# A sevenfold projection whose operand pieces, gates and sums share one ring of ten tiles, with its last two units interleaved

## The chip, the cores and the metric

The kernel runs on one core of a Trainium2 chip. The metric is the device time of one execution in microseconds, and a version is judged by the median of several executions. One more execution was taken with the hardware profiler, and the times of single instructions come from it.

## What is computed

One layer of a decoder block for 1024 tokens of width 1024 in float32. Two mixers read the same normalised input: a dilated attention, which gives `o_a`, and a retention, which gives `o_r`. Each is projected to the model's width, the two are gated and added, and an output projection and an MLP follow:

```python
y = jax.nn.sigmoid(gate_a) * (o_a @ w_proj_a[l]) + jax.nn.sigmoid(gate_b) * (o_r @ w_proj_b[l])
x = x + y @ w_out[l]
xn2 = rmsnorm(x, norm2_g[l])
x = x + jnp.square(jax.nn.relu(xn2 @ w_up[l])) @ w_down[l]
```

The change lies in the stage that computes `o_r @ w_proj_b` (2048 by 1024 weights), the second gating and the sum `y`.

## The kernel before

**Products.** Float32 accuracy is made from two halves of each operand: `split` (L320, L321) lets ScalarE copy a tile into a rounded high half (names that end in h) and VectorE subtract it for the low half (names that end in l). A product of two operands is then three matmuls for each 128 rows of the contraction, high by high and the two mixed ones. `Pipe.group` (L223) issues them; all matmuls of the trace have that line.

**Sevenfold units.** The stage multiplies by a Strassen scheme: 8 units j of 7 products N1 to N7, each of 4 contraction steps and 3 matmuls, 12 matmuls of 128x512 in all, so 56 products. Units 0 to 3 handle one half of the contraction and units 4 to 7 the other, so that unit j + 4 adds to the results of unit j. A unit gives four results of 128x512, at N2, N7, N4 and N3. `product` issues one product and what follows it. Three PSUM banks of a unit gather the sums: one in pool `mm` for N1 and N2, one in pool `ms` for N6, N7 and N4, one in `mm` for N5 and N3. Between the products stand copies that TensorE must wait for:

- after N1, ScalarE copies the negated bank to the `ms` bank (L387); N2 overwrites its bank only after that;
- after N6, ScalarE copies its bank to `u2` (L392); N7 waits for it, since it adds to that bank;
- after N7, ScalarE copies to `u3` (L395), which N4 waits for, and VectorE subtracts the third bank from `u3` (L396), which N3 waits for, since it overwrites that bank;
- after N3, VectorE subtracts `u2` from the bank (L401).

`u2` and `u3` come from the pool `pub`, one buffer each.

**Operands.** The other operand of each product, 2 x 7 sums of parts of `o_r`, was put into DRAM (`on_d`) by the stage before. The stage loads it while it runs, in pieces: `load_sum` (DMA at L786, tile `oraw`, 512 KB) requests half an operand, and `part_sum` splits it (128x1024, one instruction on ScalarE and one on VectorE). A piece is requested after each product if fewer than two are open, and split two products after its request. Pool `pr2` has two tiles. Operands for units 0 to 3: N4, N3 and for units 4 to 7: N1 are loaded first, and each product of unit 3 sets its buffer free for the next operand of units 4 to 7 (the table `after`).

**Weights.** `Weights` streams `w_pb_q` through raw tiles (L176) and splits them on ScalarE and VectorE; the sums that the scheme needs on the weights' side are VectorE's at L121.

**Results.** The gated part of the first projection, `pa`, lies in DRAM (`pa_d`). A result of units 0 to 3 is either stored as it is to `pb_d` (through a ScalarE copy if it stands in PSUM, L1020), or gated with a tile of `sg_d` and added to one of `pa_d`, then stored to `pb_d` (L1029 to L1032). Which results are stored as they are is decided by `f == i`: N2 and N7. A result of units 4 to 7 is completed with what lies in `pb_d` (L1025 to L1030), and split for the output projection (`keep`); the first of each goes by way of `yl_d` in DRAM. `fetch` requests gates and sums two results ahead, into tiles `s` of the pool `pm3`, seven tiles of 256 KB, in which a request waits for the last reader of the tile seven requests back.

**Queues.** All DMAs of the stage are issued on SyncE (SP) in program order, so a write to DRAM that waits for its data holds up the loads behind it. ScalarE and VectorE also work in the order that the scheduler fixed when the kernel was built. TensorE runs the products in the order of the list `order`: for units 0 to 5, N6, N5, (j+2, N1), N7, (j+2, N2), N4, N3; for the last two units, N6, N5, N7, N3, N4 with nothing between. Behind the stage comes the output projection (`w_out`), whose weight tiles are split into buffers that a table of numbers picks.

Of the kernel before, what the change touches and what calls it, by code (L numbers as in the profile page):

```python
# [269 lines left out]
def hybrid_block(ctx: ExitStack, tc: tile.TileContext, a: dict, out: bass.AP):  # L270
# [18 lines left out]
    sg_d = dram.tile([2, KT, P, S], F, name="sg_d")  # L289
# [67 lines left out]
    for nb in range(2):  # L357
        for u in range(4):
            W.add(a["w_out"][nb, u], (4, 3, 2, 5)[u] if nb else (2, 5, 0, 1)[u])
# [334 lines left out]
    todo = []  # L694
# [253 lines left out]
    with ExitStack() as ph:  # L948
# [35 lines left out]
        pr = pool(ph, "pr2", 2)  # L984
        pub = pool(ph, "pub", 1)
        pm3 = pool(ph, "pm3", 7)
        order = [(0, "N1"), (1, "N1"), (0, "N2"), (1, "N2")]
        for j in range(8):
            more_n = [(j + 2, name) for name in ("N1", "N2")] if j < 6 else []
            order += [(j, "N6"), (j, "N5"), *more_n[:1], (j, "N7"), *more_n[1:]]  # L990
            order += [(j, name) for name in (("N4", "N3") if j < 6 else ("N3", "N4"))]
# [4 lines left out]
        def fetch(n):  # L996

            if n >= len(results):
                return
            j, f, i = results[n]  # L1000
            d, cs = 2 * (j % 4) + f, halves()[i]
            if j < 4 and f == i:
                return
            srcs = [sg_d[1], pa_d] if j < 4 else [sg_d[1], pb_d] + [pa_d] * (f == i)
            ahead[n] = [loaded(pm3, src[d, :, cs], "s") for src in srcs]
# [35 lines left out]
        todo, unit = [(c, name, h) for c, name in ((0, "N4"), (0, "N3"), (1, "N1")) for h in range(2)], {}  # L1041
        begun = []
        fetch(0)
        fetch(1)
        for i, (j, name) in enumerate(order):
            product("pb", j, name, unit, OPB[j // 4], lambda: pub, result)
            todo += [(1, after[j, name], h) for h in range(2) if (j, name) in after]
            if begun and begun[0][0] <= i - 2:
                _, c, op, h, raw = begun.pop(0)
                part_sum(OPB[c][op], raw, h)  # L1050
            if todo and len(begun) < 2:
                begun.append((i, *todo[0], load_sum(pr, *todo.pop(0))))
            if (j, name) in free:
                u = free[j, name]
                lo, _ = halves()
                keep(u, 0, lo, late.pop(u))
            if (j, name) in fetched:
                u = fetched[j, name]
                late[u] = loaded(pm3, yl_d[u - 4], "s")
# [369 lines left out]
```

## Time and profile before

| | |
|---|---|
| median of 3 runs | 2264.69 us (2263.36 to 2267.54) |
| profiled execution | 2264.52 us, of which the span on the core is 2262.8 |
| TensorE busy | 2217.5 us, 98% of the span |
| VectorE, ScalarE, GpSimd busy | 1349.2, 1046.1, 399.4 us |
| data moved | 311.64 MB, mean 138 GB/s |

Over the whole span TensorE is all but full. The stage of the 56 products runs from 1357.52 (its first matmul) to 1529.38 (the first matmul of the output projection), 7.6% of the span, and moves 43.38 MB at a mean of 248 GB/s, so the core's DMA engines work far harder there than on average. A row of the timeline gives start, duration, engine, line, operation and tile; in square brackets stands the idle time of the engine before it and the instruction that ended it. A row of the groups gives the number of instructions, their busy time and the mean of one in ns, then the idle time before them by releaser.

### The profile page before, as it was taken

The page shows a single profiled execution, that of the slowest core. Times are in us where ns is not written, and L with a number is a line of the kernel's source. Part 1 is how long each engine was busy: PE and PEld are TensorE (multiplying, and loading weights), DVE is VectorE, ACT ScalarE, POOL GpSimd, SP SyncE. Part 2 cuts the span into 40 slices and gives each one's busy share as a digit, 9 for nine tenths or more (in the row PEclk, how much of TensorE's full clock was granted, in tenths as well). Part 3 has the DMA queues.
Part 4 walks back from the last instruction along what each step waited for, and adds up shares of the span by engine and source line. Part 5 has one row for each costly group of instructions (what it writes and reads, how often), then busy time and mean ns, then how long its engine had stood idle before and what let it go on. Part 6 is the DMA issues. An engine that isn't in the chain of part 4 may idle for free. (4 is left out here: it accounts for less than half of the span.)

```text
span 2262.8 us, 30601 instructions
## 1 busy us (share of the span) xinstructions
PE 2217.5 (98%) x10772; PEld 1897.1 (84%) x10772; DVE 1349.2 (60%) x2552; ACT 1046.1 (46%) x2334; POOL 399.4 (18%) x436
## 2 busy tenths in 40 slices
PE   8999999999999999999999999989999999899999
PEld 7999999998888888888888877778788888778777
DVE  6444545455544445558677767783855556787874
ACT  6444435345333333335555634432555555654542
POOL 1111111110000000002132220000000000587873
PEclk9999999999999999999999999999999999999999
DMA  4313232322233333353464487763345556644532
GB/s 150 97 52 106 64 92 87 92 85 99 84 111 104 108 111 109 113 178 119 128 187 121 120 268 262 262 223 135 107 133 151 152 153 199 224 152 168 178 120 103
DMA packets 247565, 311.64 MB, mean 138 GB/s; under 512 B 15090, under 2 KB 171122, under 8 KB 247411
## 3 DMA queue, kind: packets, MB, share of 16 engines
q1 hardware_dynamic: 247410, 309.69, 42.2%
q8 instruction: 84, 1.38, 0.2%
q14 instruction: 71, 0.57, 0.1%
HBM read 209.92 MB, written 99.71 MB: 137 GB/s over the span
## 5 line engine op out<-in xcount | busy, mean ns | idle before, releaser
L321 DVE TENSOR_TENSOR wl<-raw,wh 128x1024 fp32r<-128x1024 f32 (+2 forms) x290 | 318.3, 1101 | 368.8 <-ACT wh L320 367.8
L223 PE MATMUL mm<-wh,xh 128*128 128x384 f32 (+1 forms) x1226 | 481.8, 393 | 0.6 <-DVE Y L1269 0.5
L223 PE MATMUL mm<-wh,xl 128*128 128x384 f32 (+1 forms) x1226 | 438.9, 358 | 1.7 <-DVE xl L321 1.6
L223 PE MATMUL mm<-wl,xh 128*128 128x384 f32 (+1 forms) x1226 | 437.5, 357 | 0.0
L320 ACT ACTIVATE wh<-raw 128x1024 fp32r<-128x1024 f32 (+2 forms) x290 | 273.3, 945 | 348.3 <-PE ms L223 116.3
L223 PE MATMUL mm<-xh,wh 128*128 128x512 f32 x720 | 283.1, 393 | 8.8 <-DVE u L396 5.7
L223 PE MATMUL mm<-xl,wh 128*128 128x512 f32 x720 | 282.4, 392 | 1.7 <-DVE xl L321 1.7
L223 PE MATMUL ms<-xh,wh 128*128 128x512 f32 x700 | 276.7, 395 | 5.5 <-ACT u L395 2.6
L223 PE MATMUL mm<-xh,wl 128*128 128x512 f32 x720 | 282.1, 392 | 0.0
L223 PE MATMUL ms<-xl,wh 128*128 128x512 f32 x700 | 273.3, 390 | 0.0
L223 PE MATMUL ms<-xh,wl 128*128 128x512 f32 x700 | 273.1, 390 | 0.0
L223 PEld LDWEIGHTS mm<-wh,xl 128*128 128x128 f32 x1226 | 230.7, 188 | 21.9 <-DVE xl L321 2.7
L223 PEld LDWEIGHTS mm<-wh,xh 128*128 128x128 f32 x1226 | 231.8, 189 | 19.9 <-DVE Y L1269 1.3
L223 PEld LDWEIGHTS mm<-wl,xh 128*128 128x128 f32 x1226 | 232.6, 190 | 16.7
L223 PEld LDWEIGHTS mm<-xh,wh 128*128 128x128 f32 x720 | 136.4, 189 | 38.9 <-DVE u L396 6.5
L223 PEld LDWEIGHTS mm<-xl,wh 128*128 128x128 f32 x720 | 136.3, 189 | 30.2 <-DVE xl L321 2.2
L223 PEld LDWEIGHTS ms<-xh,wh 128*128 128x128 f32 x700 | 131.9, 188 | 35.3 <-ACT u L395 4.5
L223 PEld LDWEIGHTS mm<-xh,wl 128*128 128x128 f32 x720 | 136.4, 189 | 28.5
L223 PEld LDWEIGHTS ms<-xh,wl 128*128 128x128 f32 x700 | 131.8, 188 | 27.7
L223 PEld LDWEIGHTS ms<-xl,wh 128*128 128x128 f32 x700 | 131.9, 188 | 26.4 <-DVE xl L321 0.2
L334 POOL TENSOR_TENSOR ssa<-ssa,half 128x2 f32<-128x2 f32 x96 | 66.7, 695 | 426.5 <-DVE ssa L333 409.6
L872 POOL TENSOR_TENSOR st<-st,half 128x1 f32<-128x1 f32 x32 | 27.5, 858 | 646.7 <-DVE st L871 641.4
(300 smaller groups left out, 3659.3 us busy)
## 6 DMA issues: line engine op xcount, KB each, us to landing
raw<-in_w_att SPq DMA_DIRECT2D x48, 384.0 KB, 3.8
raw<-in_w_up SPq DMA_DIRECT2D x32, 512.0 KB, 3.8
h_d<-s SPq DMA_DIRECT2D x64, 256.0 KB, 4.3
raw<-in_w_down SPq DMA_DIRECT2D x32, 512.0 KB, 3.8
oraw<-on_d SPq DMA_DIRECT2D x28, 512.0 KB, 4.9
s<-sg_d SPq DMA_DIRECT2D x40, 256.0 KB, 4.1
xh<-h_d SPq DMA_DIRECT2D x11, 896.0 KB, 4.3
xl<-h_d SPq DMA_DIRECT2D x10, 896.0 KB, 4.7
```

Source lines behind the costliest of these rows:

```text
L223: self.nc.tensor.matmul(ps, x, y, start=start, stop=stop, skip_group_check=not first)
L320: nc.scalar.activation(dst_h, src, AF.Copy)
L321: nc.vector.tensor_tensor(dst_l, src, dst_h.bitcast(F), op=OP.subtract)
L334: nc.gpsimd.tensor_tensor(dst, dst, half[:, :w], op=OP.pow)
L872: nc.gpsimd.tensor_tensor(st[:, 9:10], st[:, 8:9], half[:, 0:1], op=OP.pow)
```

## The change

Four things change in this stage, and a table of numbers behind it.

- *One ring.* The pools `pr2` (two tiles of 512 KB) and `pm3` (seven tiles of 256 KB) become one `pm3` of ten tiles of 256 KB, 2.5 MB instead of 2.75. Pieces of operands, gates, sums and copies of results take its tiles in turn. `u2` gets two buffers.
- *Smaller pieces.* An operand is loaded in four pieces of 256 KB instead of two of 512 KB (36 pieces instead of 18), up to two of them requested after each product, up to six open, and split three products after the request instead of two.
- *Which results are stored as they are:* `f`, that is N7 and N4 instead of N2 and N7.
- *Order of products:* units 0 to 5 as before; of the last two, each product but for the ends now stands beside one of the other unit.
- *Behind the stage*, the first two of the four weight tiles of `w_out`'s first half swap their buffers, and the last two of its second half.

```diff
@@ -356,7 +356,7 @@
     W.add_units("pb", [a["w_pb_q"][j] for j in range(8)])
     for nb in range(2):
         for u in range(4):
-            W.add(a["w_out"][nb, u], (4, 3, 2, 5)[u] if nb else (2, 5, 0, 1)[u])
+            W.add(a["w_out"][nb, u], (4, 3, 5, 2)[u] if nb else (5, 2, 0, 1)[u])
     NU, RING = FF // 256, 10
     W.add_units("up", [a["w_up"][j] for j in range(NU)])
     NC = FF // 512
@@ -981,14 +981,19 @@
         assert not waiting
         load.close()
         YS = [XS[0, 0], XS[1, 0], ES[0], ES[1]]
-        pr = pool(ph, "pr2", 2)
         pub = pool(ph, "pub", 1)
-        pm3 = pool(ph, "pm3", 7)
+
+        class parts:
+            @staticmethod
+            def tile(shape, dtype, name):
+                return pub.tile(shape, dtype, name=name, bufs=2 if name == "u2" else 1)
+
+        pm3 = pool(ph, "pm3", 10)
         order = [(0, "N1"), (1, "N1"), (0, "N2"), (1, "N2")]
-        for j in range(8):
-            more_n = [(j + 2, name) for name in ("N1", "N2")] if j < 6 else []
-            order += [(j, "N6"), (j, "N5"), *more_n[:1], (j, "N7"), *more_n[1:]]
-            order += [(j, name) for name in (("N4", "N3") if j < 6 else ("N3", "N4"))]
+        for j in range(6):
+            order += [(j, "N6"), (j, "N5"), (j + 2, "N1"), (j, "N7"), (j + 2, "N2"), (j, "N4"), (j, "N3")]
+        order += [(6, "N6"), (6, "N5"), (6, "N7"), (7, "N6"), (6, "N4"), (7, "N5"), (7, "N7"), (6, "N3"), (7, "N4"),
+                  (7, "N3")]
         results = [(j, *{"N2": (0, 0), "N7": (1, 1), "N4": (1, 0), "N3": (0, 1)}[name])
                    for j, name in order if name in ("N2", "N7", "N4", "N3")]
         ahead, late = {}, {}
@@ -999,9 +1004,9 @@
                 return
             j, f, i = results[n]
             d, cs = 2 * (j % 4) + f, halves()[i]
-            if j < 4 and f == i:
+            if j < 4 and f:
                 return
-            srcs = [sg_d[1], pa_d] if j < 4 else [sg_d[1], pb_d] + [pa_d] * (f == i)
+            srcs = [sg_d[1], pa_d] if j < 4 else [sg_d[1], pb_d] + [pa_d] * f
             ahead[n] = [loaded(pm3, src[d, :, cs], "s") for src in srcs]
 
         def keep(j, f, cs, y):
@@ -1038,18 +1043,23 @@
         after = {(3, "N1"): "N2", (3, "N2"): "N6", (3, "N6"): "N5", (3, "N5"): "N7", (3, "N7"): "N4", (3, "N4"): "N3"}
         free = {(3, "N3"): 4, (7, "N1"): 5, (7, "N2"): 6, (7, "N6"): 7}
         fetched = {order[order.index(at) - 3]: u for at, u in free.items()}
-        todo, unit = [(c, name, h) for c, name in ((0, "N4"), (0, "N3"), (1, "N1")) for h in range(2)], {}
+        todo, unit = [(c, name, k) for c, name in ((0, "N4"), (0, "N3"), (1, "N1")) for k in range(4)], {}
         begun = []
+
+        def load_part(c, name, k):
+
+            return loaded(pm3, on_d[2 * c + k // 2, 2 * SUMS.index(name) + k % 2], "s")
+
         fetch(0)
         fetch(1)
         for i, (j, name) in enumerate(order):
-            product("pb", j, name, unit, OPB[j // 4], lambda: pub, result)
-            todo += [(1, after[j, name], h) for h in range(2) if (j, name) in after]
-            if begun and begun[0][0] <= i - 2:
-                _, c, op, h, raw = begun.pop(0)
-                part_sum(OPB[c][op], raw, h)
-            if todo and len(begun) < 2:
-                begun.append((i, *todo[0], load_sum(pr, *todo.pop(0))))
+            product("pb", j, name, unit, OPB[j // 4], lambda: parts, result)
+            todo += [(1, after[j, name], k) for k in range(4) if (j, name) in after]
+            while begun and begun[0][0] <= i - 3:
+                _, c, op, k, raw = begun.pop(0)
+                split(*(x[:, k] for x in OPB[c][op]), raw)
+            while todo and len(begun) < 6 and (len(begun) < 2 or begun[-2][0] < i):
+                begun.append((i, *todo[0], load_part(*todo.pop(0))))
             if (j, name) in free:
                 u = free[j, name]
                 lo, _ = halves()
```

The order of the instructions on the engines follows from the program and the scheduler. Three places are shown.

ScalarE where the stage begins, before. `wh_...` are high halves of weights, `xh` those of operands, `raw_...` raw weights, and `ms<-mm` the copy after N1, here of units 0 and 1:

```order
L320 ACTIVATE wh_13264<-raw_12828 128x512
L320 ACTIVATE wh_13264<-raw_13046 128x512
L320 ACTIVATE xh<-oraw 128x1024
L320 ACTIVATE wh_13310<-raw_12828 128x1024
L320 ACTIVATE wh_13306<-raw_12962 128x1024
L320 ACTIVATE xh<-oraw 128x1024
L387 ACTIVATE ms<-mm 128x512 x2
L320 ACTIVATE wh_13392<-raw_13108 128x1024
```

The same place in the changed kernel:

```order
L320 ACTIVATE wh_13264<-raw_12828 128x512
L320 ACTIVATE wh_13264<-raw_13046 128x512
L320 ACTIVATE wh_13310<-raw_12828 128x1024
L320 ACTIVATE wh_13306<-raw_12962 128x1024
L387 ACTIVATE ms<-mm 128x512
L320 ACTIVATE wh_13401<-raw_13108 128x1024
L387 ACTIVATE ms<-mm 128x512
L320 ACTIVATE wh_13391<-raw_13316 128x1024
L320 ACTIVATE xh<-s 128x512 x4
L392 ACTIVATE u_13448<-ms 128x512
```

The two operand splits that stood ahead of the copies now stand behind them, as four smaller ones, and one weight split stands between the two copies.

ScalarE where unit 4 begins, in the changed kernel, with the tiles' numbers. `s_13988` is a tile from `yl_d`, `s_14035` the copy of (3, N4)'s result, `s_14048` and `s_14050` are the last pieces of operand N4, `s_14080` to `s_14106` the four pieces of N3, `ms_14138` the copy after unit 6's N1:

```order
L320 ACTIVATE xh_92<-s_13988 128x512
L1025 ACTIVATE s_14035<-ms_13638 128x512
L320 ACTIVATE xh_98<-s_14048 128x512
L320 ACTIVATE wh3_14072<-raw3_13828 128x1024
L392 ACTIVATE u2_14098<-ms_13804 128x512
L320 ACTIVATE xh_98<-s_14050 128x512
L320 ACTIVATE xh_13061<-s_14080 128x512
L320 ACTIVATE xh_13061<-s_14082 128x512
L320 ACTIVATE xh_13061<-s_14104 128x512
L387 ACTIVATE ms_14138<-mm_14125 128x512
```

And SP's queue there, in the changed kernel:

```order
L1026 DMA pb_d_88<-s_14035 128x512
L779 DMA s_14048<-on_d_85 128x512
L779 DMA s_14050<-on_d_85 128x512
L779 DMA s_14065<-sg_d_82 128x512
L779 DMA s_14067<-pb_d_88 128x512
L779 DMA s_14080<-on_d_85 128x512
L1037 DMA pb_d_88<-s_14004 128x512
L779 DMA s_14082<-on_d_85 128x512
L779 DMA s_14104<-on_d_85 128x512
L779 DMA s_14106<-on_d_85 128x512
```

The write of the copied result, which was not there for N4 before, now stands ahead of the loads of six pieces, and the splits of five of these stand ahead of the copy after unit 6's N1.

ScalarE's copies out of PSUM in the last two units, before:

```order
L392 ACTIVATE u_14365<-ms 128x512
L320 ACTIVATE wh_14349<-raw_14117 128x1024
L320 ACTIVATE xh<-s 128x512
L320 ACTIVATE wh_14404<-raw_14115 128x1024
L395 ACTIVATE u_14392<-ms 128x512
L320 ACTIVATE xh<-s 128x512
L320 ACTIVATE wh_14435<-raw_14274 128x1024
L320 ACTIVATE wh_14520<-raw_14408 128x1024
L320 ACTIVATE xh<-s 128x512 x3
L392 ACTIVATE u_14473<-ms 128x512
```

The same in the changed kernel:

```order
L392 ACTIVATE u_14430<-ms 128x512
L320 ACTIVATE wh_14414<-raw_14176 128x1024
L320 ACTIVATE xh<-s 128x512
L320 ACTIVATE wh_14473<-raw_14174 128x1024
L395 ACTIVATE u_14459<-ms 128x512
L320 ACTIVATE xh<-s 128x512
L392 ACTIVATE u_14491<-ms 128x512
L320 ACTIVATE xh<-s 128x512
L320 ACTIVATE wh_14588<-raw_14477 128x1024
L320 ACTIVATE xh<-s 128x512
L320 ACTIVATE wh_14555<-raw_14337 128x1024
L395 ACTIVATE u_14541<-ms 128x512
```

The copy after unit 7's N6 (the second L392) now follows unit 6's copy of N7 with one split between them, where five splits in three rows stood before; the two copies of `u2` fall closer together, as the second has its own buffer.

## The prediction

> **What bounds the kernel now.** I read the view that sums the engines over stretches of time first, for the stage of the 56 products:
>
> ```profile
> core 0: us, PE busy (x) PEld busy (x) DVE busy (x) ACT busy (x) POOL busy (x), PEclk, DMA share, GB/s
> 1357.50:1375.00 17.50, 14.99 (x59) 11.86 (x58) 15.63 (x19) 10.21 (x13) 0.00 (x0) 0.90 0.81 271
> 1375.00:1440.00 65.00, 64.87 (x287) 53.39 (x286) 42.66 (x54) 26.20 (x33) 0.00 (x0) 1.00 0.75 251
> 1440.00:1470.00 30.00, 26.79 (x116) 21.17 (x115) 23.07 (x29) 14.56 (x18) 0.00 (x0) 1.00 0.82 286
> 1496.00:1529.00 33.00, 26.25 (x101) 20.51 (x100) 24.57 (x33) 12.96 (x17) 0.00 (x0) 0.90 0.62 203
> ```
>
> TensorE is the bound: full from 1375 to 1440, with holes at the start, around unit 4 and in the last two units. VectorE and ScalarE have room in every row (VectorE 15.63 of 17.50 us at the start), DMA is three quarters to four fifths busy. How long the stage would be without holes follows from TensorE's own rows, in order of time:
>
> ```profile
> 1357.52 0.39 PE L223 MATMUL mm<-xh,wh 128*128 128x512 f32 x1
> 1362.73 0.39 PE L223 MATMUL mm<-xh,wl 128*128 128x512 f32 x1
> 1365.63 0.50 PE L223 MATMUL mm<-xh,wh 128*128 128x512 f32 x1 [2.51 <-ACT ms L387]
> 1366.71 0.63 PE L223 MATMUL mm<-xl,wh 128*128 128x512 f32 x1
> 1370.08 0.40 PE L223 MATMUL mm<-xh,wh 128*128 128x512 f32 x1
> 1444.65 0.50 PE L223 MATMUL ms<-xh,wh 128*128 128x512 f32 x1 [0.49 <-ACT u L395]
> 1461.91 0.50 PE L223 MATMUL mm<-xh,wh 128*128 128x512 f32 x1 [0.63 <-ACT ms L387]
> 1467.02 0.50 PE L223 MATMUL ms<-xh,wh 128*128 128x512 f32 x1 [2.10 <-ACT u L395]
> 1498.36 0.50 PE L223 MATMUL ms<-xh,wh 128*128 128x512 f32 x1 [1.08 <-ACT u L392]
> 1504.23 0.50 PE L223 MATMUL mm<-xh,wh 128*128 128x512 f32 x1 [2.84 <-DVE u L396]
> 1520.98 0.80 PE L223 MATMUL mm<-xh,wh 128*128 128x512 f32 x1 [2.84 <-DVE u L396]
> 1527.09 0.39 PE L223 MATMUL ms<-xh,wl 128*128 128x512 f32 x1
> 1529.38 0.39 PE L223 MATMUL mm<-wh,xh 128*128 128x512 f32 x1
> ```
>
> The first two products are 24 matmuls, whose starts run from 1357.52 to 1362.73: a step of 5.21 / 23 = 0.227 us, 2.72 us a product. The stage's 56 x 12 = 672 matmuls would take 152.3 us; the next stage's first matmul starts at 1529.38, 171.9 us after the first. So **19.5 us** are lost, and the rows name them (each idle time costs 0.16 more than it says, since a matmul lasts 0.39 where the step is 0.227):
> - start: 2.51 idle, then slow matmuls: the 8 from 1366.71 to 1370.08 take 3.37 where 8 steps are 1.81, and the clock column stands at 0.90. With 0.2 of slow restart 4.4.
> - middle: 0.49 + 0.63 + 2.10 + 3 x 0.16 = 3.7.
> - end: 1.08 + 2.84 + 2.84 + 3 x 0.16 = 7.2, and the 14 steps from 1520.98 to 1527.09 take 6.11 for 3.17: 2.9 more. Together 10.2.
>
> These make 18.3; the other 1.2 is in hitches of up to 0.4 us. Nine tenths of the loss thus stand in seven waits and the two slow stretches behind the longest. The views of waits, of TensorE and of ScalarE in this stage, say on whom:
>
> ```profile
> PE mm L223 <- DVE u L396: 5.7, 2, 2.8
> PE mm L223 <- ACT ms L387: 3.1, 2, 2.5
> ACT xh L320 <- DMA oraw<-on_d: 21.4, 12, 3.8
> ACT u L392 <- DVE s L1029: 11.8, 5, 5.8
> ```
>
> TensorE waits for copies out of PSUM (L387, L392, L395) that stand in ScalarE's queue behind a split that waits for a piece of an operand: 12 such waits of up to 3.8 us. The fourth row is the one u2 buffer: the copy of N6 waits for the reader of the last unit's u2.
>
> **The start.** ScalarE's rows of before, at the first hole:
>
> ```profile
> 1359.68 1.06 ACT L320 ACTIVATE xh<-oraw 128x1024 fp32r<-128x1024 f32 x1 [3.76 <-DMA oraw<-on_d]
> 1362.31 1.06 ACT L320 ACTIVATE wh<-raw 128x1024 fp32r<-128x1024 f32 x1 [0.62 <-DVE raw L121]
> 1364.04 1.06 ACT L320 ACTIVATE xh<-oraw 128x1024 fp32r<-128x1024 f32 x1 [0.67 <-DMA oraw<-on_d]
> 1365.00 1.06 ACT L387 ACTIVATE ms<-mm 128x512 f32<-128x512 f32 x2
> ```
>
> The copies for products 3 and 4 start at 1365.00, behind the second operand split; TensorE follows 0.63 us behind (1365.63). In the changed order no operand split stands ahead of them: two weight splits, copy, weight split, copy. The first split now waits for L121 alone, whose results freed it at 1362.31 in before; the two splits end about 1363.9 and the copy follows, TensorE at 1364.58: idle about 1.45. The second copy has another weight split ahead of it that waits for VectorE's sums (L121) of the next raw tile; laid along VectorE's order I get (1, N2) at 1368.2, 0.95 late. No slow stretch is counted, since no idle time of 0.49 to 2.10 in the rows above is followed by one. With restarts 2.8, against 4.4: **1.6 won**. The bounds: all 4.4, or nothing, if the pieces come later. They may, for the N2 of units 0, 1 and 2 are now among the results that are gated at once: two loads of 256 KB each, 1.5 MB called for at the start, where the DMA engines were 0.81 busy at 271 GB/s.
>
> The Trainium skill ("TensorE: Matmul & The Clock Gate", Part 1, "What's actually happening") has the clock fall only after at least one window of about 3.4 us without work. The trace differs: an idle 2.51 and one 2.84 were followed by slow matmuls, another 2.84 (1504.23) was not; the slow stretch of 3.37 has the page's length. By the page's rule none of these waits is long enough, so the slow 1.6 and 2.9 would have another cause and might stay: 4.5 less gain.
>
> **The middle.** What delays the copies there, and what the pieces cost:
>
> ```profile
> 1465.43 1.06 ACT L320 ACTIVATE xh<-oraw 128x1024 fp32r<-128x1024 f32 x1 [2.59 <-DMA oraw<-on_d]
> 1466.39 0.58 ACT L395 ACTIVATE u<-ms 128x512 f32<-128x512 f32 x1
> oraw<-on_d SPq DMA_DIRECT2D x17, 512.0 KB, 4.9
> s<-sg_d SPq DMA_DIRECT2D x25, 256.0 KB, 4.2
> L320 ACT ACTIVATE xh<-s 128x512 fp32r<-128x512 f32 x14 | 8.7, 628 | 17.5 <-DVE s L1027 9.2 <-DVE s L1030 6.1 <-PE ms L223 1.6
> L321 DVE TENSOR_TENSOR xl<-s,xh 128x512 fp32r<-128x512 f32 x14 | 9.4, 684 | 1.6 <-ACT xh L320 1.6
> L320 ACT ACTIVATE xh<-oraw 128x1024 fp32r<-128x1024 f32 x18 | 19.1, 1060 | 27.7 <-DMA oraw<-on_d 21.4 <-PE ms L223 3.7 <-PE mm L223 2.5
> L321 DVE TENSOR_TENSOR xl<-oraw,xh 128x1024 fp32r<-128x1024 f32 x18 | 22.0, 1221 | 16.9 <-ACT xh L320 15.6 <-PE ms L223 1.3
> ```
>
> Thirty-six small pieces take the place of 18: ScalarE 36 x 0.628 - 18 x 1.060 = 3.5 us more, VectorE 36 x 0.684 - 18 x 1.221 = 2.6 more, over 170 us in which both idle longer: nothing on the path, up to 0.5 where a copy is queued right behind. A piece is now split three groups (8.2 us) behind its request against 5.4, and lands in about 4.2: the wait of 2.59 in the first row, and its likes, go. In their place comes the ring. Gates, sums and pieces take its ten tiles in turn, so a load waits for the reader of the tile ten requests back, and SP issues in order. I laid the changed orders of ScalarE, SP and the ring along TensorE's steps. Up to unit 3 I find nothing late. Where unit 4 begins, in turn: the split of yl_d's tile waits for the last product of (3, N3), since it writes where that product reads; behind it on ScalarE stands the copy of (3, N4)'s result (+0.75 us); on that waits SP's write to pb_d (+1.4); behind the write on SP stand the last pieces of N4 (issued +1.75, landed by 4.2 us +5.9), and their split frees the tiles of N3's pieces (issued +7.45, landed +11.6); ScalarE takes those before the copy of unit 6's N1, which then starts at +12.2 with TensorE at +12.8, where (6, N2) is due 4 products behind, at +10.9. **A new wait of about 2.0**, from 0.5 to 3.7 if each of the two loads lands 0.8 sooner or later. Behind it I count 0.35 for (4, N4), 0.25 for (7, N2), 0.25 for (1, N4), and 0.7 for a slow stretch (1.6 with a chance of 0.4): 3.55 against 3.7, **0.15 won**. Bounds: 3.7 won, or 3 lost.
>
> The Trainium skill ("DMA: Bandwidth & Descriptors", "Bandwidth") wants transfers of 1 MiB or more for three quarters of the peak, which speaks against halving the pieces. The rows agree in kind, 256 KB taking 4.2 us where 512 KB take 4.9; where loads follow one another that is 8.4 us a half megabyte against 4.9, and the chain above, with two loads in it, is dearer for it.
>
> **The end.** Why TensorE waits there:
>
> ```profile
> 1497.71 0.60 ACT L392 ACTIVATE u<-ms 128x512 f32<-128x512 f32 x1 [2.43 <-DVE s L1029]
> 1501.26 1.06 ACT L320 ACTIVATE wh<-raw 128x1024 fp32r<-128x1024 f32 x1 [1.43 <-PE ms L223]
> 1502.23 0.58 ACT L395 ACTIVATE u<-ms 128x512 f32<-128x512 f32 x1
> 1503.49 0.68 DVE L396 TENSOR_TENSOR u<-u,mm 128x512 f32<-128x512 f32 x1
> ```
>
> The chain behind N7 is a weight split, the copy L395, then L396 behind that split's other half; it ends 0.7 us after 1503.49, and N3, the very next product, needs it. In both last units that costs 2.84. The change puts another product between N7 and its readers N4 and N3: (7, N6) after (6, N7), (6, N3) after (7, N7). It gives 2.72 us of cover; N4 needs the copy alone, which was over before 1503.49, and N3, which needs L396 too, has two or more products ahead of it where the chain was 2.84 long. The wait at 1498.36 is for the u2 buffer, which has a second one now; Followed product by product, the least slack is 0.9 us, at the copy of (7, N7), whose queue holds a split of w_out's first tiles; w_out's own first matmul has 0.7. With 0.3 for a late one, 10.2 - 0.3 = **9.9 won**, the slow stretch of 2.9 included, since the idle time ahead of it goes. Bounds: 10.2, or 6 if the copy of (7, N7) is late by a split of w_out and its 1.06 us bring a slow stretch with them.
>
> **Sum.** 1.6 + 0.15 + 9.9 = 11.65, less 0.65 for splits that fall ahead of a copy: 11.0. The profiled execution, 2264.52 (span 2262.8 and 1.7 around it), becomes 2253.5; it lies 0.2 below the median, 2264.69, which becomes **2253.7**. What follows the stage keeps its order on TensorE, VectorE and ScalarE, but its idle times of up to 4 us may meet or miss a slow stretch: 1.6 to 2.9 either way.
>
> **The rivals.**
> - *Only the end is won.* The early gate loads fill the DMA engines (0.81 busy), pieces come late at the start as before, and the ring costs 1.5 to 3 more than the waits that go in the middle: 9.9 less that, 2256 to 2258. For it speaks the DMA share, against it that three groups leave 4 us beyond a landing. 0.20.
> - *All is hidden.* The new wait is covered because loads land sooner than the median; 16 to 18.3 won, 2246 to 2249. For it: a stretch of 65 us almost without a hole in before, with seven tiles. 0.12.
> - *The slow stretches stay.* The waits go, but the clock falls for another reason than idle time: 11.0 less 1.6 and 2.9 is 6.5, so 2258.2. For it: the second 2.84 without a slow stretch; against: each stretch begins within 1.1 us of the end of an idle time of over 2.5. The rule on the clock gate cited above would give this. 0.06.
> - *The ring starves, slower.* One mechanism: the copy of a product's result (L1025) stands behind a late split on ScalarE, SP's write to pb_d holds all loads behind it, the next pieces are late, and so the next split. If it recurs at each of the 8 results that units 0 to 3 store (their N7 and N4) rather than once, each costs the 2.0 above and 1.7 of slow matmuls: 29.6; with all of before's 18.3 gone, 2264.7 - 18.3 + 29.6 = 2276. It decides from five times on (5 x 3.7 = 18.5). For it: SP's one queue in order; against: in units 0 to 2 I find no piece late. 0.09.
> - *The change doesn't do what it says:* the order on the engines is set when the kernel is built and might put pieces ahead of the copies as before. The built order shows the copies ahead at the start and the new order at the end; what would be left is 2262 to 2267, the waits of before give or take a load. 0.05.
>
> The forecast has the other 0.48. **How the numbers follow.** The likeliest case by itself spans 2249 to 2259 (bounds of the middle and of later slow stretches). The range 2247 to 2264 takes in the rivals that are faster than before, but for the best of *all is hidden*, and leaves the starved ring out. 0.2% is 4.5 us, about what a measurement can tell from no change: 2260.2 and 2269.2. Faster than that: 0.48 x 0.94 + 0.20 x 0.85 + 0.12 + 0.06 x 0.9 = 0.79; slower: the starved ring and a little of the last, 0.10; the rest 0.11.
>
> **What would show it.** Right: no idle time over 1 us for L396 or L392 in the last two units, the clock there at 1.00; a first idle time near 1.5 for L387; one idle time near 2 for L387 at unit 6's N1, with loads of pieces ahead of it. Wrong: that wait absent (all hidden) or repeated in units 1 to 5 (starved), or the next stage's first tile late.

## The result, and the profile after

The changed kernel takes 2254.61 us (median of 9 runs, 2252.0 to 2260.11) where before takes 2263.85 in the same runs; the ratio is 0.9957, with a 95% interval of 0.9947 to 0.9968, so 7.2 to 12.0 us less. The forecast was 2253.7. Its profiled execution has a span of 2250.3 us, at 2252.05 one of its fastest.

The view that sums the engines over stretches, of the changed kernel's stage; columns as before:

```profile
1357.12:1375.00 17.88, 15.16 (x66) 11.86 (x65) 14.72 (x21) 6.50 (x9) 0.00 (x0) 1.00 0.72 246
1375.00:1440.00 65.00, 63.42 (x279) 51.86 (x278) 47.87 (x67) 31.58 (x49) 0.00 (x0) 1.00 0.78 259
1440.00:1470.00 30.00, 29.81 (x132) 24.37 (x131) 24.39 (x35) 16.51 (x26) 0.00 (x0) 1.00 0.82 288
1470.00:1496.00 26.00, 25.25 (x112) 20.57 (x111) 23.38 (x38) 9.73 (x16) 0.00 (x0) 1.00 0.77 257
1496.00:1516.54 20.54, 20.54 (x92) 17.00 (x91) 17.02 (x23) 9.83 (x15) 0.00 (x0) 1.00 0.64 218
1516.54:1529.00 12.46, 10.85 (x47) 8.36 (x46) 9.50 (x13) 3.37 (x5) 0.00 (x0) 1.00 0.63 225
```

The last 20 us of the stage are full (20.54 busy of 20.54) at the whole clock, where before the last 33 us had 6.75 idle and a clock of 0.90. New holes are in the second row (63.42 of 65.00 for 64.87), in the fourth (25.25 of 26.00) and in the last one, which is the start of the output projection. TensorE's rows with an idle time, and the first matmul of each stage:

```profile
1357.12 0.39 PE L223 MATMUL mm<-xh,wh 128*128 128x512 f32 x1
1364.79 0.50 PE L223 MATMUL mm<-xh,wh 128*128 128x512 f32 x1 [2.07 <-ACT ms L387]
1368.47 0.50 PE L223 MATMUL mm<-xh,wh 128*128 128x512 f32 x1 [0.66 <-ACT ms L387]
1404.39 0.50 PE L223 MATMUL ms<-xh,wh 128*128 128x512 f32 x1 [0.23 <-ACT u L395]
1422.36 0.50 PE L223 MATMUL mm<-xh,wh 128*128 128x512 f32 x1 [1.36 <-ACT ms L387]
1460.94 0.50 PE L223 MATMUL mm<-xh,wh 128*128 128x512 f32 x1 [0.19 <-ACT ms L387]
1481.03 0.50 PE L223 MATMUL mm<-xh,wh 128*128 128x512 f32 x1 [0.75 <-ACT ms L387]
1516.54 0.39 PE L223 MATMUL mm<-wh,xh 128*128 128x512 f32 x1
1522.73 0.50 PE L223 MATMUL mm<-wh,xh 128*128 128x512 f32 x1 [1.26 <-ACT xh L320]
1523.80 0.50 PE L223 MATMUL mm<-wh,xl 128*128 128x512 f32 x1 [0.34 <-DVE xl L321]
```

The stage lasts 1516.54 - 1357.12 = 159.4 us for 171.9, a loss of 7.1 over the 152.3 of its matmuls. Dividing the time between the waits by 2.72 tells the products: the waits are at (0,N2) and (1,N2), then (1,N4), (4,N2), (6,N2) and (7,N2), and none in the last two units. The output projection's first group runs seven of its eight contraction steps (21 matmuls from 1516.54) and then waits 1.26 and 0.34. Up to the next transposes on TensorE it takes 58.6 us where before took 56.5, which is 2.2 more before rounding. So 12.4 - 2.2 = 10.2 come from the places that the change touches. The span is 12.5 shorter; the other 2.3 lie ahead of the stage and far behind it.

### The profile page after: what moved, and what is told of

It reads as the page before. It is cut to its first block, busy times and chain, and to the rows that moved or that the text cites. A ratio compares the mean times of both kernels' runs of the same rounds, so it can differ in the third digit from the quotient of the medians.

```text
span 2250.3 us, 30678 instructions
## 1 busy us (share of the span) xinstructions
PE 2211.8 (98%) x10772; PEld 1893.1 (84%) x10772; DVE 1351.1 (60%) x2570; ACT 1047.8 (47%) x2352; POOL 398.6 (18%) x436
## 5 line engine op out<-in xcount | busy, mean ns | idle before, releaser
L321 DVE TENSOR_TENSOR wl<-raw,wh 128x1024 fp32r<-128x1024 f32 (+2 forms) x290 | 317.4, 1097 | 366.5 <-ACT wh L320 365.4
```

The costliest lines, as they stand in the source:

```text
L321: nc.vector.tensor_tensor(dst_l, src, dst_h.bitcast(F), op=OP.subtract)
```

## The experiments

Each ratio is to the kernel before on the same chip; the changed kernel's is 0.9957. The stage is the time from its first matmul to the output projection's in the run's profiled execution.

| run | ratio (95%) | stage |
|---|---|---|
| changed | 0.9957 (0.9947 to 0.9968) | 159.4 |
| old order of the last two units | 0.9986 (0.9975 to 0.9996) | 166.8 |
| only the new order | 0.9968 (0.9955 to 0.9981) | 164.2 |
| N2 and N7 stored | 0.9957 (0.9940 to 0.9974) | 163.9 |
| writes on GpSimd | 0.9976 (0.9966 to 0.9986) | 166.7 |
| (7,N4) earlier | 0.9950 (0.9936 to 0.9965) | 159.8 |
| split after two products | 0.9960 (0.9945 to 0.9975) | 161.4 |
| split after four | 0.9956 (0.9941 to 0.9971) | 159.6 |
| old table for w_out | 0.9953 (0.9937 to 0.9970) | 163.8 |
| N1 earlier | 0.9944 (0.9930 to 0.9957) | 155.8 |
| N1 and (7,N4) earlier | 0.9942 (0.9927 to 0.9958) | 158.3 |
| the same, other start | 0.9945 (0.9932 to 0.9957) | 156.9 |
| changed, again | 0.9959 (0.9945 to 0.9972) | 160.9 |

### The change in two halves

The changed kernel with the old order at the end:

```diff
-        for j in range(6):
-            order += [(j, "N6"), (j, "N5"), (j + 2, "N1"), (j, "N7"), (j + 2, "N2"), (j, "N4"), (j, "N3")]
-        order += [(6, "N6"), (6, "N5"), (6, "N7"), (7, "N6"), (6, "N4"), (7, "N5"), (7, "N7"), (6, "N3"), (7, "N4"),
-                  (7, "N3")]
+        for j in range(8):
+            more_n = [(j + 2, name) for name in ("N1", "N2")] if j < 6 else []
+            order += [(j, "N6"), (j, "N5"), *more_n[:1], (j, "N7"), *more_n[1:]]
+            order += [(j, name) for name in (("N4", "N3") if j < 6 else ("N3", "N4"))]
```

> The changed kernel with the last two units in their old order (N6, N5, N7, N3, N4 of unit 6, then of unit 7); ring, small pieces and both u2 buffers stay. Theory 1 (the gain is the new order of the last two units): TensorE waits 2.8 for L396 in both last units again and a slow stretch of about 3 may follow, and the 2.4 that the output projection loses at its start goes: 2254.6 + 9.0 - 2.4 = 2261.2. Theory 2 (the gain is the ring and the small pieces, which bring operands and gates earlier): within 1 of the changed kernel, 2254 to 2256.

Its view of waits for TensorE, over the last two units:

```profile
PE mm L223 <- DVE u L396: 5.7, 2, 2.8
```

The row is before's, to the tenth: both waits of 2.84 for L396 are back, and the stage loses 14.5 us instead of 7.1. The ratio of 0.9986 is 3.2 us below before, where 2.7 were expected of theory 1. But the output projection still waits 1.34 at its start, which by theory 1 was to go. That wait is therefore not made by the new order alone.

The other half, in the kernel before (with the class `parts` of the change, so that `u2` has two buffers):

```diff
-        pm3 = pool(ph, "pm3", 7)
+        pm3 = pool(ph, "pm3", 6)
...
-            order += [(j, name) for name in (("N4", "N3") if j < 6 else ("N3", "N4"))]
+        order += [(6, "N6"), (6, "N5"), (6, "N7"), (7, "N6"), (6, "N4"), (7, "N5"), (7, "N7"), (6, "N3"), (7, "N4"),
+                  (7, "N3")]
```

> The kernel before with the new order of the last two units and the second u2 buffer alone; large pieces in their own pool, old table of the output projection; the pool of gates has six tiles instead of seven, to make room for the second u2. Theory 1: the start (4.4) and the middle (3.7) lose as before, the end loses nothing, the output projection's start up to 2.4: 2263.9 - 10.2 + 2.4 = 2256.1. Theory 2: 2262 or more.

The ratio of 0.9968 is 7.3 us; 7.8 were expected. Start and middle wait as in before (2.58 for L387, 0.58 and 3.52 for L395 in its trace), and at the end only 0.32 is left, for a low half of weights. The longest is

```profile
1468.56 0.50 PE L223 MATMUL ms<-xh,wh 128*128 128x512 f32 x1 [3.52 <-ACT u L395]
```

The two halves add up within the intervals, 3.2 + 7.3 = 10.5 where the whole gives 9.7: about seven tenths of the gain are the order of ten products, three tenths the ring with its small pieces and the rest. The second `u2` buffer is in both halves and so counts twice; the wait of 1.08 for L392, which before has in unit 6, stands in neither trace, and no run has that buffer alone. Theory 2 falls.

### What is left in the middle

The largest wait left there is the 1.36 at (4,N2), for the copy after N1. First the results that are stored as they are, chosen as before:

```diff
-            if j < 4 and f:
+            if j < 4 and f == i:
...
-            srcs = [sg_d[1], pa_d] if j < 4 else [sg_d[1], pb_d] + [pa_d] * f
+            srcs = [sg_d[1], pa_d] if j < 4 else [sg_d[1], pb_d] + [pa_d] * (f == i)
```

> The changed kernel, but units 0 to 3 store N2 and N7 as they are, as before, instead of N7 and N4. Theory A (the late piece behind the wait at unit 4's N2 is held on SP by the write of the copied N4): that wait of 1.4 and the one at unit 1's N4 go, the middle loses about 1.5 instead of 3.6: 2252.5. Rival B (any write of a result holds SP's loads, or the ring does): the waits move to other products, the middle loses 3 to 4 and the time is within 1 of 2254.6.

The wait at unit 4's N2 is gone, but 0.49 stands at the N2 of unit 5 and 2.74 at unit 4's N4, with slow matmuls behind it, and the ratio is the changed kernel's: rival B. Which results are stored as they are moves waits and wins nothing that can be measured. At the output projection's start this run waits once, for 0.85.

Next the writes of results, issued on GpSimd:

```diff
-                nc.sync.dma_start(pb_d[2 * j + f, :, cs], y)
+                nc.gpsimd.dma_start(pb_d[2 * j + f, :, cs], y)
...
-                nc.sync.dma_start(yl_d[j - 4], y)
+                nc.gpsimd.dma_start(yl_d[j - 4], y)
```

(both writes to `pb_d`)

> The changed kernel, with the stage's writes of results to DRAM issued on GpSimd, which does nothing else in this stage, instead of on SP, so that no load stands behind a write. Theory A (SP held by writes): the pieces and the weight load behind the wait at unit 4's N2 are issued 1 to 3 us earlier, the waits at the N2 of units 4 and 7 go, the middle loses about 1 instead of 3.6: 2252. Rival B (loads wait for tiles of the ring or of the raw weights): the same waits within 0.5, 2254.6.

Worse than the changed kernel by 4 us, though the two intervals just touch. Waits for L387 come larger and at other units, 1.99 at (2,N2) and 1.91 at (3,N2). The second of them in ScalarE's rows of this run:

```profile
1409.73 1.06 ACT L320 ACTIVATE wh<-raw 128x1024 fp32r<-128x1024 f32 x1 [3.04 <-DMA raw<-in_w_pb_q]
1410.70 0.58 ACT L387 ACTIVATE ms<-mm 128x512 f32<-128x512 f32 x1
```

No write stands ahead of a load on SP here, and still the copy is behind a split of weights that waits for its load: moving the writes does not take the waits away, as theory A had it. But this run doesn't clear SP's queue or the ring. A stored result landed 5.2 us after its issue here for 3.6 in the changed kernel, and its tile of the ring is free only then: over the stage, SP's loads into the ring waited 17.0 us for such writes to `pb_d` (1.2 in the changed kernel) and 13.1 for those to `yl_d` (3.1), with the loads of weights in the same queue behind them. So the write that held the loads by its place in the queue now holds them by its tile, for longer. Two runs on the pieces' delay:

```diff
-            while begun and begun[0][0] <= i - 3:
+            while begun and begun[0][0] <= i - 2:
```

> The changed kernel with the pieces split two products behind their request, as before, instead of three. Theory A (the third product of delay is what keeps late pieces from standing ahead of the copies on ScalarE): pieces land in 5.0 at the median, two products are 5.4, so the late half stands ahead of copies again, the middle loses 2 to 4 more, ratio 0.9965 to 0.9975. Rival B (the order of the queue, not the delay, decides): within 0.001 of the changed kernel's 0.9957.

> The changed kernel with the pieces split four products behind their request. Theory A (pieces that come late because SP was held are what is left in the middle): the wait of 1.4 at unit 4's N2 goes, the middle loses 1 to 2 instead of 3.6, ratio 0.995. Rival B (the ring is what is scarce): pieces hold their tiles 2.7 longer, loads of gates and of the next pieces come later, and the middle loses 3 to 6, ratio 0.9957 to 0.997.

(The second has `i - 4`. In it some products read parts of an operand before their last pieces are split, so that they multiply old data; the work is the same.) Neither time moves. The trace with two products has waits of 0.49 and 0.65 at unit 4's N7 and unit 6's N2 (the changed kernel none and 0.19), and a longer one at the start, 3.08; with four, the wait at unit 4's N2 stands at 1.21 and that of unit 7's has grown to 1.46. Theory A falls in both runs: the delay is not what limits. Rival B of the second, whose range begins at the changed kernel's ratio, is not excluded. Where unit 4's N2 waits, the copy stands behind a split of weights in every trace, and that split waits for its load, for 3 to 5 us. ScalarE's, VectorE's and SP's rows of the changed kernel, one fence each:

```profile
1413.17 0.63 ACT L320 ACTIVATE xh<-s 128x512 fp32r<-128x512 f32 x1 [4.84 <-DMA s<-on_d]
1413.70 1.05 ACT L320 ACTIVATE wh<-raw 128x1024 fp32r<-128x1024 f32 x1
...
1420.76 1.06 ACT L320 ACTIVATE wh<-raw 128x1024 fp32r<-128x1024 f32 x1 [3.67 <-DMA raw<-in_w_pb_q]
1421.73 0.58 ACT L387 ACTIVATE ms<-mm 128x512 f32<-128x512 f32 x1
```

```profile
1415.04 1.22 DVE L321 TENSOR_TENSOR wl<-raw,wh 128x1024 fp32r<-128x1024 f32 x1
```

```profile
1416.29 8.61 SPq L176 DMA_DIRECT2D raw<-in_w_pb_q  x2
```

The load of weights is issued at 1416.29, when VectorE's subtract of 1415.04 (it ends at 1416.26) has given a raw tile back; 4.5 us later the split of what it brought begins, and the copy follows. Here a late piece (4.84) had delayed the subtract; with four products of delay no split of a piece stood ahead of it, the load was issued 57.7 us after the stage's start instead of 59.2, but the split of what it brought began 5.9 us later instead of 4.5, and TensorE still waited 1.21. What the copy stands behind is the stream of weights through its raw tiles; over the stage, SP's loads of weights waited 32.7 us for VectorE's subtracts, more than for anything else. That more raw tiles or sooner landings would take the wait away is argued and not tested. If the copy's place is what costs, it has to leave that place, or the product that waits for it:

```diff
-            order += [(j, "N6"), (j, "N5"), (j + 2, "N1"), (j, "N7"), (j + 2, "N2"), (j, "N4"), (j, "N3")]
+            order += [(j, "N6"), (j + 2, "N1"), (j, "N5"), (j, "N7"), (j + 2, "N2"), (j, "N4"), (j, "N3")]
```

> The changed kernel with N1 of unit j+2 one product earlier in units 0 to 5: N6, (j+2,N1), N5, N7, (j+2,N2), N4, N3, so that two products instead of one stand between N1 and the N2 that waits for its copy. Theory A (what is left in the middle are copies after N1 that stand on ScalarE behind a split of weights whose load waits for one of the four raw tiles; it recurs at the N2 of every unit, 0.2 to 1.6 late, in all versions so far): 2.7 more cover hides all of them, the waits for L387 after the start go, 2.5 to 3.5 less in the stage, ratio 0.9943. Rival B (ScalarE's order shifts with the products, so that the copy stands as late as before, or N1 itself waits for its weights): the waits move to N7, N4 or N1, ratio within 0.001 of 0.9957.

TensorE's waits in its stage, and ScalarE at the place shown above:

```profile
PE mm L223 <- ACT ms L387: 1.8, 2, 1.1
PE ms L223 <- ACT u L395: 0.3, 1, 0.3
```

```profile
1418.71 0.59 ACT L387 ACTIVATE ms<-mm 128x512 f32<-128x512 f32 x1
1422.33 2.01 ACT L320 ACTIVATE wh<-raw 128x1024 fp32r<-128x1024 f32 x2 [3.03 <-DMA raw<-in_w_pb_q]
```

The waits go as theory A has it: both for L387 that are left (1.15 and 0.66) are at the start, none in the middle, and the stage loses 3.5 instead of 7.1. The two later runs with this order have none for L387 in the middle either. The split still waits for its load of weights (3.03), but the copy, whose product ends 2.7 us earlier, now stands ahead of it. The ratio is 0.9944; 0.9943 was expected, though its interval reaches the changed kernel's 0.9957.

### The two ends

```diff
-        order += [(6, "N6"), (6, "N5"), (6, "N7"), (7, "N6"), (6, "N4"), (7, "N5"), (7, "N7"), (6, "N3"), (7, "N4"),
-                  (7, "N3")]
+        order += [(6, "N6"), (6, "N5"), (6, "N7"), (7, "N6"), (7, "N5"), (7, "N7"), (6, "N4"), (7, "N4"), (6, "N3"), (7, "N3")]
```

> The changed kernel with the last two units laid into each other in another way: (6,N6) (6,N5) (6,N7) (7,N6) (7,N5) (7,N7) (6,N4) (7,N4) (6,N3) (7,N3), so that (7,N4), whose result the output projection needs in its first group, ends two products before the last instead of one. Theory A (the idle 1.3 and 0.3 at the output projection's start come from the gating of (7,N4), which stands on VectorE behind splits of w_out): that wait goes and nothing new comes in the last two units, 2254.6 - 2.2 = 2252.4 against the before of 2263.9, a ratio of 0.995. Rival B (w_out's weights themselves are late, whichever result is last): the wait stays at 1.5 to 2.5, the ratio 0.9957 of the changed kernel.

The wait for the operand at the output projection's start is gone, and 0.68 for the low half of a tile of w_out (L321) is there in its place, in this trace and with 0.68 and 0.77 in both later ones with this order. So A names the larger part and B a remainder. The ratio is as A expected, but 0.7 in a thousand better than the changed kernel is within both intervals. VectorE's rows of the changed kernel, which A was read from:

```profile
1517.79 1.22 DVE L321 TENSOR_TENSOR wl<-raw,wh 128x1024 fp32r<-128x1024 f32 x1
1518.93 0.68 DVE L1030 TENSOR_TENSOR s<-s,ms 128x512 f32<-128x512 f32 x1
1519.53 0.68 DVE L401 TENSOR_TENSOR u<-mm,u 128x512 f32<-128x512 f32 x1
1520.13 0.68 DVE L1031 TENSOR_TENSOR s<-s 128x512 f32<-128x512 f32 x1
1520.73 0.68 DVE L1034 TENSOR_TENSOR s<-s,u 128x512 f32<-128x512 f32 x1
1521.33 0.68 DVE L1032 TENSOR_TENSOR s<-s 128x512 f32<-128x512 f32 x1
```

(7,N4) ended at about 1514, but its result is completed (L1030 to L1032) from 1518.93 on, behind a split of w_out and with the work on (7,N3) between, and ScalarE's split of it begins at 1522.04. Before has two instructions there, the multiplication by the gate (L1029) when the matmuls have ended, and one of the two additions of the second row (the other is (7,N3)'s):

```profile
1529.59 0.69 DVE L1029 TENSOR_TENSOR s<-s,ms 128x512 f32<-128x512 f32 x1 [0.59 <-PE ms L223]
1530.19 1.29 DVE L1030 TENSOR_TENSOR s<-s 128x512 f32<-128x512 f32 x2
```

The third instruction of the changed kernel is the sum with `pa`, which N4 needs in units 4 to 7 since units 0 to 3 now store it as it is.

The old table of buffers for w_out, in the changed kernel:

```diff
-            W.add(a["w_out"][nb, u], (4, 3, 5, 2)[u] if nb else (5, 2, 0, 1)[u])
+            W.add(a["w_out"][nb, u], (4, 3, 2, 5)[u] if nb else (2, 5, 0, 1)[u])
```

> The changed kernel with the old table of buffers for w_out's tiles. Theory A (the table decides when w_out's first splits can run): with the old one the first tile waits for a buffer that a later product frees, the idle time at the output projection's start grows from 1.6 to 3 or more, ratio 0.9965. Rival B (the splits wait for loads and for VectorE, not for buffers): within 0.001 of 0.9957.

Rival B in the time. In the trace the wait changes its object, from an operand to the weights (0.54 and 0.81, 1.35 in sum where 1.60 stood). The table is worth nothing that can be measured here. But the trace shows something else. ScalarE's order in the stage is the changed kernel's, and still its copies after N1 are waited for at the N2 of units 2, 4, 5, 6 and 7, for 0.50, 1.54, 0.79, 0.83 and 1.58, and the stage takes 163.8 instead of 159.4. So one profile does not tell the size of these waits, and differences of a few us between the stages in the table are not results by themselves.

N1 earlier and the other order of the last two units together:

> The kernel of the run before (N1 one product earlier) with the other order of the last two units too: (6,N6) (6,N5) (6,N7) (7,N6) (7,N5) (7,N7) (6,N4) (7,N4) (6,N3) (7,N3). If the two are independent, it adds what that order alone gave (0.995 against 0.9957, 1.5 us): ratio 0.9937, 2250 where before is 2264. If the gain of that order was noise: the same as the run before.

0.9942 where 0.9937 was expected: no more than N1 earlier gives alone. Its trace has no wait for L387 in the middle, but 1.21 at (0,N4) and 0.55 at (4,N4) for L395: in part, the waits have moved to N4.

```diff
-        order = [(0, "N1"), (1, "N1"), (0, "N2"), (1, "N2")]
+        order = [(0, "N1"), (1, "N1"), (0, "N5"), (0, "N2"), (1, "N2")]
```

(and the product taken out of unit 0's list)

> The kernel of the run before with the start's order changed too: (0,N1) (1,N1) (0,N5) (0,N2) (1,N2) (0,N6) and so on, so that a product which waits for no copy out of PSUM stands between (1,N1) and (0,N2). Theory A (the wait of 2.1 at (0,N2) is for the copy behind two splits of weights, and 2.7 more cover hides it and the 0.7 behind it): 2.5 to 4 less, with the slow stretch that some runs show there; ratio 0.992. Rival B ((0,N5) itself waits for its weight tile, which is split after the ones before it): the wait moves to (0,N5), ratio as in the run before.

No wait is left at (0,N2) and (1,N2), as theory A has it; but TensorE now waits at (0,N7), and at (0,N4) as in the run before:

```profile
1378.84 0.50 PE L223 MATMUL ms<-xh,wh 128*128 128x512 f32 x1 [1.50 <-ACT u L392]
1385.71 0.50 PE L223 MATMUL ms<-xh,wh 128*128 128x512 f32 x1 [1.13 <-ACT u L395]
```

The start's waits moved by some products and the ratio stays at 0.9945. That is neither theory as it was put: (0,N5) did not wait.

### Once more

> The changed kernel itself a second time, with a second profile, to tell what of its waits recurs. If the waits are set by the order of the queues: L387 at unit 4's N2 (1.4) and unit 7's N2 (0.8), L387 twice at the start (1 to 2.5, and 0.7), the split of the operand at the output projection's start (1.3 and 0.3), each within 0.5 of the first profile, none over 1 us in another place, and no waits in the last two units; ratio 0.9957, above the 0.9944 of the version with N1 one product earlier. If they are accidents of the transfers: other products, and the ratio may lie at 0.9944 as well.

```profile
PE mm L223 <- ACT ms L387: 4.8, 3, 1.8
PE mm L223 <- ACT xh L320: 1.3, 1, 1.3
PE ms L223 <- ACT u L395: 0.5, 1, 0.5
```

Of the waits of the first profile, those at (0,N2), (1,N4), (4,N2), (7,N2) and the output projection's start are there again (1.80, 0.51, 1.49, 1.53, and 1.30 with 0.35), and its trace marks no other wait. That speaks for the order of the queues, but only for where they wait: (7,N2) is 0.8 longer, outside the 0.5 that was expected, (1,N2) did not wait, and a slow stretch stood at the start. With the old table for w_out, the same order on ScalarE had further places.

Of the versions that were run, N1 one product earlier has the shortest stage and, with the two versions built on it, the lowest ratios: 12.7 us under before. Over the changed kernel it gains 3 us by the ratios, but their intervals overlap (0.9930 to 0.9957 and 0.9947 to 0.9968), so that this gain is likely and not shown.

## Why the prediction held, and where it did not

**The sum: right, in part by luck.** 11.0 were forecast, and the ratio gives 9.7, from 7.2 to 12.0. Counted by the starts of the matmuls in the two profiles, the start gave 1.1 where 1.6 were forecast, the middle 0.8 for 0.15, and the end 10.5, of which the output projection took 2.2 back: 8.3 for 9.9. Together that is 10.2, against 11.65 less the 0.65 set aside for splits ahead of a copy. The terms are off by up to 1.6 and partly cancel. Of the signs that were named, those of the last two units came true. The wait of about 2 for the copy after unit 6's N1 is 0.19, and its absence had been named as a sign of being wrong; so had a late start of the next stage, which came by an operand and not by its first tile.

**The end: right, and the largest term.** 9.9 were to be won; 10.2 were lost there by the prediction's rows, 10.5 by the starts of the matmuls, and nothing is lost now. The run with the old order has the two waits for L396 back, the run with the new one alone is without them. That an idle time taken away takes its slow stretch along fits too: the clock column stands at 1.00 in the last two units.

**The output projection's start: missed by 2.2.** The slack of 0.7 for "w_out's own first matmul" held for that matmul; the step failed to follow the group to its last contraction step, whose operand comes from (7,N4), and to count the third instruction that this result now takes on VectorE. Moving (7,N4) forward takes the wait for the operand away, and with N2 and N7 stored as before, so with two instructions, 0.85 was left of 1.6. Both halves of the change lose time there by themselves (1.34 with the old order; 1.27 and 0.76 with the new order alone, for weights). How much of it each of the three has, the ring, the order and the stored results, was not taken apart further.

**The start: right in kind, its loss put too small by 0.6.** The first copy was to start at 1363.9 and started at 1364.16, and TensorE was done with (1,N1) 0.4 earlier, as the stage began earlier: 2.07 idle instead of 1.45. The second wait was to be 0.95 and was 0.66. By the starts of the matmuls, restarts included, 3.4 were lost against the 2.8 of the sum. In the second profile it was one wait of 1.80 and a slow stretch, 3.7 in all, and no slow stretch had been counted.

**The middle: right as a sum, by two errors against each other.** 3.55 were expected, and by the starts of the matmuls 3.8 are lost, 4.9 in the second profile; before lost 4.6 there, counted the same way, where the sum had the 3.7 of its waits alone. The wait of 2.0 at (6,N2) is 0.19. Its whole chain is in the trace, in the order that the prediction gave. ScalarE's rows of the changed kernel:

```profile
1447.87 0.63 ACT L320 ACTIVATE xh<-s 128x512 fp32r<-128x512 f32 x1 [0.27 <-PE mm L223]
1448.41 0.58 ACT L1025 ACTIVATE s<-ms 128x512 f32<-128x512 f32 x1
1455.01 0.63 ACT L320 ACTIVATE xh<-s 128x512 fp32r<-128x512 f32 x1 [6.03 <-DMA s<-on_d]
...
1459.14 1.26 ACT L320 ACTIVATE xh<-s 128x512 fp32r<-128x512 f32 x2 [0.85 <-DMA s<-on_d]
1460.31 0.58 ACT L387 ACTIVATE ms<-mm 128x512 f32<-128x512 f32 x1
```

From the split of yl_d's tile to the copy after unit 6's N1 it takes 12.4 us; 12.2 were forecast. The step that failed is "the split of yl_d's tile waits for the last product of (3, N3)". TensorE's rows there:

```profile
1446.99 0.39 PE L223 MATMUL mm<-xh,wh 128*128 128x512 f32 x1
1447.21 0.39 PE L223 MATMUL mm<-xl,wh 128*128 128x512 f32 x1
1447.44 0.39 PE L223 MATMUL mm<-xh,wl 128*128 128x512 f32 x1
1447.67 0.39 PE L223 MATMUL mm<-xh,wh 128*128 128x512 f32 x1
```

(3,N3) runs from 1446.99 to 1449.7. The split begins at 1447.87, when its first three matmuls are done: it overwrites one quarter of the operand, and only these read that quarter. So the chain began 1.8 us earlier than was assumed (1449.7 less 1447.87), and that is what the wait is short of. In its place stand the waits at the N2 of units 4 and 7, 1.36 and 0.75, of which the second was put at 0.25 and the first falls under "Up to unit 3 I find nothing late". The traces show the copy there behind a split that waits for its load of weights, which the prediction's account of the middle does not name.

The landing time was also put too low: 4.2 us for a piece of 256 KB was read from the loads of gates in before. In the changed kernel the pieces took 5.0 us at the median, as long as the pieces of 512 KB before (4.9), so that halving them did not bring them sooner.

**The rivals.** The starved ring does not appear in the changed kernel: in units 0 to 3 its trace has one wait in the middle beside that at (4,N2), 0.23. With the writes on GpSimd the loads do wait for tiles of the ring, and the time is 4 us longer. Not all is hidden, since 7.1 are still lost. The slow stretches went with the waits in the first profile, whose clock column is 1.00 throughout; the second has one at the start again, behind an idle time. That only the end is won comes closest of the rivals by its price, 2256 to 2258, but not by its reason: start and middle gained 1.1 and 0.8.

## What to carry to other kernels

A wait of the matrix engine for a short copy is often not about the copy but about what its engine has queued ahead; putting one more product between a copy and its reader was worth more here (7.3 us, with the second buffer that run has) than the common ring with its smaller loads (3.2). When such waits go, follow the next stage to the last operand of its first group, not to its first matmul. And before a wait "for a product" is put into a sum, look which part of the tile is overwritten: the wait ends with the last matmul that reads this part.

## What the runs showed of the hardware

The length of an idle time did not decide whether slow matmuls follow. In the changed kernel's first profile 2.07 at the start was not followed by any, in its second 1.80 was:

```profile
1367.72 0.55 PE L223 MATMUL mm<-xh,wh 128*128 128x512 f32 x1 [1.80 <-ACT ms L387]
1368.06 0.63 PE L223 MATMUL mm<-xl,wh 128*128 128x512 f32 x1
...
1371.46 0.40 PE L223 MATMUL mm<-xh,wh 128*128 128x512 f32 x1
```

And with the old table for w_out not even 2.58 was:

```profile
1368.08 0.50 PE L223 MATMUL mm<-xh,wh 128*128 128x512 f32 x1 [2.58 <-ACT ms L387]
1368.41 0.39 PE L223 MATMUL mm<-xl,wh 128*128 128x512 f32 x1
```

The stretch itself again lasted 3.4 us (1368.06 to 1371.46). The Trainium skill ("TensorE: Matmul & The Clock Gate", Part 1, "What's actually happening") calls its window of about 3.4 us free-running, and a window that runs on by itself would make the same idle time count or not by where it falls; the lengths agree with that. But this page of the Trainium skill asks for a whole window without work, and of the idle times with slow matmuls behind them only the 3.52 with the new order alone was that long. The prediction's ground for counting no slow stretch at the start, that no idle time of up to 2.10 had been followed by one, was therefore too few cases: behind an idle time of 1.8 to 2.8 a slow stretch may follow or not, and it has to be counted with a probability.
